# The modulation of the first norm on TensorE from row tiles of its weights, and ordinary products for the first query and key groups

## The chip, the cores and the metric

One core of a Trainium2 chip runs the whole program. The metric is device time in microseconds (us), the median of three runs. All arrays are 32-bit floats in HBM; a sequence of 512 tokens with 1024 channels goes through two transformer blocks.

## The reference, cut to what matters

Only the beginning of the first block bears on the change.

```
mod = silu(c) @ w_ada + b_ada                       # c: 1 x 1024, w_ada: 1024 x 6144
shift1, scale1, gate1, shift2, scale2, gate2 = split(mod, 6)
hmix = rmsnorm(x, g_norm1) * (1 + scale1) + shift1  # x: 512 x 1024
proj = hmix @ w_in                                  # w_in: 1024 x 11264
sb_q, sb_k, sb_v, r_q, r_k, r_v, r_g, br = split(proj, ...)   # sb_*: 1024 columns each, 16 heads of 64
```

After it come the stick-breaking attention over the 16 heads, a retention mixer, the projections, a feed-forward layer, and then the whole second block. Of `mod`, the first norm needs `shift1` and `scale1` alone: columns 0 to 2047 of `w_ada`, 8 MB.

## The kernel before, in words

Activations lie transposed: 8 tiles of 128 channels by 512 tokens. A product with a weight matrix is made in higher precision from three products (`mm3`): each operand is split into a rounded part (`hi`, made by ScalarE with a copy) and the rest (`lo`, made by a subtraction), and hi·hi, hi·lo and lo·hi are added up in PSUM. `weights` (line 167) loads 512 KB of a weight matrix (4 tiles of 128 rows, 256 columns) on SP's queue, ScalarE makes `wh` and VectorE `wl`. `gemm` (line 189) makes 256 output columns from two such loads: 2 x 8 x 3 = 48 products of 128x128 weights with 512 tokens, for the first output tile and then for the second within each load.

The beginning is written differently. It wants the first products under way while the 8 MB of `w_ada` still arrive, so it goes by channel tiles k = 0 to 7 (`arrive`, line 337). For each k it loads the 128 columns of `shift1` and the 128 of `scale1` that belong to this channel tile, all 1024 rows of them, together with the rows k of `w_in` for six output tiles: query columns 0 to 511 and key columns 0 to 255 (lines 341 and 342). `ada_part` (line 322) multiplies the 8 row tiles by `silu(c)` and adds them up on VectorE, 8 instructions of 128x256 for each k; `ada_total` (line 331) sums over the partitions with two one-column products on TensorE. A program line of TensorE with plain 32-bit operands becomes two instructions, each with its own weight load, so these are four in the trace. `modulated` (line 424) turns the sums into a factor and a shift and makes the two halves of the normed tile H[k]; for k of 2 and up GpSimd has multiplied x by the reciprocal root (`x_norm`, line 449). `w_split` (line 440) splits the rows of `w_in`: ScalarE makes the hi part, GpSimd the lo part. Then all 6 x 3 products with H[k] are issued, into six PSUM accumulators that stay open over all k (lines 467 to 469). The query tiles 0 to 3 (two groups of 256 columns) and the key tiles 0 and 1 (one group) are done when k = 7 is through.

Before that, x is loaded in four tiles of 128 tokens and turned by 32 transposes on TensorE (`x_turn`, line 350; four of the eight channel tiles before the norm's reciprocal roots are spread over the partitions, four after). The sums of squares are taken on ScalarE and VectorE, the power on GpSimd, and `spread` (line 268) makes R0 on TensorE.

After the six accumulators are emptied (`q_stack`, `k_stack`), the attention loop over the heads starts (line 617). Into it a queue of background products (`Feed`) is interleaved: the value groups, the other query and key groups and the gates. How much is put between two steps of the loop is set by hand in us (`SB_FILL`). All instructions are placed in their engines' queues when the program is built, by a scheduler that goes by the order in the program and by estimated readiness; on the chip every engine works through its own queue in that order.

Loads go through SP's queue in the order of issue. A store of x to HBM (`xspill`, 8 x 256 KB) is held until the last load of the beginning has been issued (line 474).

The steps of the prediction touch: `ada_load` (284), `ada_part` (322), `ada_total` (331), `arrive` (337), `x_turn` (350), `modulated` (424), `w_split` (440), `x_norm` (449), the loop of the first pass (459), the emptying of the accumulators (568) and the filling of the background queue (573).

Of the kernel before, what the change touches and what calls it, by code (L numbers as in the profile page):

```python
# [74 lines left out]
X_EARLY = 4  # L75
N_DIRECT = 2
# [45 lines left out]
def build(tc, A, dump=None):  # L122
    nc = tc.nc
    with ExitStack() as es:
# [64 lines left out]
        def gemm(w, kt, c0, X, evac, n0=0, k0w=0, tag="g"):  # L189

            ps = [psum(tag) for _ in range(2)]
            for b, kn in ksteps(kt, 4):
                wh, wl = weights(w, k0w + b, kn, c0, 256)
                for n, i in ((n, i) for i in range(kn) for n in range(2)) if kt == 4 else \
                        ((n, i) for n in range(2) for i in range(kn)):
                    s, k = slice(n * 128, n * 128 + 128), b + i
                    mm3(ps[n], wh[:, i, s], wl[:, i, s], X[k][0], X[k][1], b + i == 0, b + i == kt - 1)
                    if b + i == kt - 1:
                        evac(n0 + n, ps[n])
                    yield STEP  # L200
# [81 lines left out]
        w_ada4 = A["w_ada"].rearrange("(k p) (g n) -> p k g n", p=128, n=D)  # L282

        def ada_load(k, k0):

            tag = "raw" if k0 == 0 or k % 2 == 0 else "q" if k == 1 else "wl"
            n = 2 if tag == "q" else 4
            rows = []
            for j in range(k0, k0 + 4, n):
                raw = (new(tag) if n == 2 else wtile(tag, [128, 1024], F32)).rearrange("p (k n) -> p k n", n=256)  # L290
                for g in range(2):
                    nc.sync.dma_start(raw[:, :, g * 128:g * 128 + 128], w_ada4[:, j:j + n, g, k * 128:(k + 1) * 128])
                rows += [raw[:, i] for i in range(n)]
            return rows

        xr = []
        first = ada_load(0, 0)
# [39 lines left out]
        def arrive(k):  # L337

            raws = (first if k == 0 else ada_load(k, 0)) + ada_load(k, 4)
            wr = [new("q"), new("q")]  # L340
            nc.sync.dma_start(wr[0], w_in[k * 128:(k + 1) * 128, 0:512])
            last = nc.sync.dma_start(wr[1][:, 0:256], w_in[k * 128:(k + 1) * 128, 1024:1280])
            acc = new("t")[:, 0:256]
            ada_part(raws, acc)
            return acc, wr, last

        coming = [arrive(0)]
# [10 lines left out]
        for k in range(X_EARLY):  # L358
# [15 lines left out]
        for k in range(X_EARLY, KD):  # L374
            x_turn(k)
# [44 lines left out]

        H = []
        a1 = small("a1", 8)
        acc = [psum("g") for _ in range(3)] + [psum("z") for _ in range(2)] + [psum("r")]
        def modulated(k):
            ps = ada_total(coming[k][0])
            nc.vector.tensor_add(mod[:, k:k + 1], ps[:, 0:1], col("b_ada", k))
            nc.vector.scalar_tensor_tensor(out=a1[:, k:k + 1], in0=ps[:, 1:2], scalar=bsc1[:, k:k + 1],
                                           in1=col("g_norm1", k), op0=ALU.add, op1=ALU.mult)
            H.append(pair("p"))
            if k < N_DIRECT:  # L430
                norm_mod(xT[k], R0, a1[:, k:k + 1], mod[:, k:k + 1], H[k])
                return
            t = new("t")
            nc.scalar.activation(t, xn[k], AF.Identity, scale=a1[:, k:k + 1], bias=mod[:, k:k + 1])
            split(t, *H[k])

        xn = {}
        ws = {}

        def w_split(k):  # L440
            wr = coming[k][1]
            wh = wtile("wh", [128, 1024], F32R)
            wl = wtile("wl", [128, 1024], F32R)
            for r, o, n in ((wr[0], 0, 512), (wr[1], 512, 256)):
                nc.scalar.copy(wh[:, o:o + n], r[:, 0:n])
                nc.gpsimd.tensor_tensor(out=wl[:, o:o + n], in0=r[:, 0:n], in1=f(wh[:, o:o + n]), op=ALU.subtract)
            ws[k] = wh, wl

        def x_norm(k):
            if k >= N_DIRECT:  # L450
                xn[k] = new("p")
                nc.gpsimd.tensor_tensor(out=xn[k], in0=xT[k], in1=R0, op=ALU.mult)

        x_norm(0)
        w_split(0)
        modulated(0)
        x_norm(1)
        coming.append(arrive(1))
        for k in range(KD):
            if k + 2 < KD:  # L460
                coming.append(arrive(k + 2))
                x_norm(k + 2)
            if k + 1 < KD:
                w_split(k + 1)
                modulated(k + 1)
            wh, wl = ws[k]
            for n, off in enumerate((0, 128, 512, 640, 256, 384)):
                s = slice(off, off + 128)
                mm3(acc[n], wh[:, s], wl[:, s], H[k][0], H[k][1], k == 0, k == KD - 1)
        last_load = coming[-1][2]  # L470
# [97 lines left out]
        for n in (0, 1):  # L568
            ev_q(n, acc[n])
            ev_k(n, acc[2 + n])  # L570
        for n in (4, 5):
            ev_q(n, acc[n])
        for g in range(4):
            if g > 1:
                bg.add("qk%d" % g, gemm(w_in, KD, 256 * g, H, ev_q))
            if g > 0:
# [858 lines left out]
```

## Time and profile before

| | |
|---|---|
| median of 3 runs | 1952.21 us (1951.51 to 1953.27) |
| the profiled execution, its own time | 1956.69 us |
| its span (first to last instruction) | 1955.0 us |
| TensorE busy (PE) | 1879.9 us, 96% |
| weight loads (PEld, beside PE) | 1563.7 us, 80% |
| VectorE (DVE) / ScalarE (ACT) / GpSimd (POOL) | 1062.4 / 748.5 / 287.9 us |

The profile names engines PE (matrix products), PEld (weight loads of TensorE, which overlap PE), DVE, ACT, POOL and SP; a name with q is an engine's queue. A row of a timeline gives the start in us, the busy time in us, engine, line, operation, output<-inputs and, after x, how many instructions were merged. A bracket gives the idle time before it and what ended it. Ends of products are modelled and overlap, so the distance between starts is the pace, and not the duration shown. TensorE's clock has two levels, 1.2 and 2.4 GHz; PEclk is the granted share of the higher one.

### The profile page before, as it was taken

The page shows a single profiled execution, that of the slowest core. Times are in us where ns is not written, and L with a number is a line of the kernel's source. Part 1 is how long each engine was busy: PE and PEld are TensorE (multiplying, and loading weights), DVE is VectorE, ACT ScalarE, POOL GpSimd, SP SyncE. Part 2 cuts the span into 40 slices and gives each one's busy share as a digit, 9 for nine tenths or more (in the row PEclk, how much of TensorE's full clock was granted, in tenths as well). Part 3 has the DMA queues.
Part 4 walks back from the last instruction along what each step waited for, and adds up shares of the span by engine and source line. Part 5 has one row for each costly group of instructions (what it writes and reads, how often), then busy time and mean ns, then how long its engine had stood idle before and what let it go on. Part 6 is the DMA issues. An engine that isn't in the chain of part 4 may idle for free. (4 is left out here: it accounts for less than half of the span.)

```text
span 1955.0 us, 24601 instructions
## 1 busy us (share of the span) xinstructions
PE 1879.9 (96%) x9561; PEld 1563.7 (80%) x9561; DVE 1062.4 (54%) x1732; ACT 748.5 (38%) x1248; POOL 287.9 (15%) x361
## 2 busy tenths in 40 slices
PE   6889999999999999999999999979999899999998
PEld 4678887888989898888888888858888788888886
DVE  6888876645565555655334422467577554433222
ACT  3466654233332323333322222474366542223122
POOL 3232221102030302010000002122234200000000
PEclk7999999999999999999999999979999999999999
DMA  6612122533424243623333233266453123333222
GB/s 214 204 55 66 61 70 86 162 125 103 131 84 143 79 130 114 212 84 97 97 97 91 93 106 109 71 162 151 98 136 113 44 76 97 90 94 97 86 86 75
DMA packets 196400, 209.73 MB, mean 107 GB/s; under 512 B 10038, under 2 KB 179012, under 8 KB 196284
## 3 DMA queue, kind: packets, MB, share of 16 engines
q1 hardware_dynamic: 189920, 188.48, 31.6%
q0 software_dynamic: 6016, 19.57, 4.2%
q8 instruction: 75, 1.23, 0.3%
q14 instruction: 41, 0.34, 0.1%
q10 hardware_dynamic: 348, 0.13, 0.0%
HBM read 189.25 MB, written 9.99 MB: 102 GB/s over the span
## 5 line engine op out<-in xcount | busy, mean ns | idle before, releaser
L160 PE MATMUL ps_g<-p,wh 128*128 128x512 f32 (+1 forms) x1464 | 579.4, 399 | 9.3 <-DVE q L943 3.7
L161 PE MATMUL ps_g<-p,wh 128*128 128x512 f32 (+1 forms) x1464 | 576.3, 394 | 2.8 <-DVE p L415 2.8
L162 PE MATMUL ps_g<-p,wl 128*128 128x512 f32 (+1 forms) x1464 | 575.5, 394 | 0.0
L183 DVE TENSOR_TENSOR wl<-raw,wh 128x1024 fp32r<-128x1024 f32 (+1 forms) x262 | 325.9, 1244 | 447.8 <-ACT wh L182 446.6
L182 ACT CAST wh<-raw 128x1024 fp32r<-128x1024 f32 (+1 forms) x262 | 273.2, 1043 | 630.5 <-PE ps_g L161 358.3
L160 PEld LDWEIGHTS ps_g<-p,wh 128*128 128x128 f32 x1464 | 276.4, 190 | 75.1 <-issue 8.3
L162 PEld LDWEIGHTS ps_g<-p,wl 128*128 128x128 f32 x1464 | 277.2, 189 | 63.4
L161 PEld LDWEIGHTS ps_g<-p,wh 128*128 128x128 f32 x1464 | 277.4, 190 | 62.2 <-DVE p L415 3.6
L213 PE MATMUL ps_g<-wh,p 128*128 128x256 f32 x512 | 147.3, 288 | 2.0 <-ACT wh L182 1.5
L214 PE MATMUL ps_g<-wl,p 128*128 128x256 f32 x512 | 144.3, 282 | 1.2 <-DVE wl L183 1.2
L215 PE MATMUL ps_g<-wh,p 128*128 128x256 f32 x512 | 144.7, 283 | 0.0
L160 PE MATMUL ps_g<-q,wh 128*128 128x512 f32 (+1 forms) x368 | 141.7, 388 | 0.2 <-DVE p L1269 0.2
L162 PE MATMUL ps_g<-q,wl 128*128 128x512 f32 (+1 forms) x368 | 141.5, 385 | 0.0
L161 PE MATMUL ps_g<-q,wh 128*128 128x512 f32 (+1 forms) x368 | 141.5, 385 | 0.0
L213 PEld LDWEIGHTS ps_g<-wh,p 128*128 128x128 f32 x512 | 97.9, 191 | 3.3 <-ACT wh L182 1.9
L214 PEld LDWEIGHTS ps_g<-wl,p 128*128 128x128 f32 x512 | 97.9, 191 | 1.9 <-DVE wl L183 1.4
L215 PEld LDWEIGHTS ps_g<-wh,p 128*128 128x128 f32 x512 | 97.7, 191 | 0.1
L160 PEld LDWEIGHTS ps_g<-q,wh 128*128 128x128 f32 x368 | 69.1, 188 | 16.1 <-DVE p L1269 0.6
L162 PEld LDWEIGHTS ps_g<-q,wl 128*128 128x128 f32 x368 | 69.2, 188 | 15.0
L161 PEld LDWEIGHTS ps_g<-q,wh 128*128 128x128 f32 x368 | 69.2, 188 | 14.5
L150 ACT CAST q<-t 128x512 fp32r<-128x512 f32 (+1 forms) x68 | 39.1, 581 | 87.3 <-DVE t L890 48.8
L329 DVE SCALAR_TENSOR_TENSOR adaacc<-raw,cact,adaacc 128x256 f32<-128x256 f32 x112 | 53.9, 482 | 23.9 <-DMA raw<-in_w_ada 22.1
(376 smaller groups left out, 2600.7 us busy)
## 6 DMA issues: line engine op xcount, KB each, us to landing
raw<-in_w_in SPq DMA_DIRECT2D x108, 512.0 KB, 3.9
raw<-in_w_ffn_in SPq DMA_DIRECT2D x44, 512.0 KB, 3.4
raw<-in_w_ada SPq DMA_DIRECT2D x32, 512.0 KB, 3.4
raw<-in_w_ffn_gate SPq DMA_DIRECT2D x22, 512.0 KB, 3.7
raw<-in_w_ffn_up SPq DMA_DIRECT2D x22, 512.0 KB
raw<-in_w_ffn_down SPq DMA_DIRECT2D x22, 512.0 KB, 3.6
wl<-raw POOLq DMA_DIRECT2D x20, 512.0 KB, 5.6
raw<-in_w_ffn_out SPq DMA_DIRECT2D x19, 512.0 KB, 3.5
```

The costliest lines, as they stand in the source:

```text
L150: nc.scalar.copy(hi, src)
L160: nc.tensor.matmul(ps, lh, rh, start=start, stop=False)
L161: nc.tensor.matmul(ps, lh, rl, start=False, stop=False)
L162: nc.tensor.matmul(ps, ll, rh, start=False, stop=stop)
L182: nc.scalar.copy(wh, raw)
L183: low_engine["e"].tensor_tensor(out=wl, in0=raw, in1=f(wh), op=ALU.subtract)
L213: nc.tensor.matmul(o, xh[:, ts], wh[:, i], start=k == 0 and t % 2 == 0, stop=False)
L214: nc.tensor.matmul(o, xh[:, ts], wl[:, i], start=False, stop=False)
L215: nc.tensor.matmul(o, xl[:, ts], wh[:, i], start=False, stop=k == KD - 1 and t % 2 == 1)
L329: nc.vector.scalar_tensor_tensor(out=acc, in0=w, scalar=c, in1=acc, op0=ALU.mult, op1=ALU.add)
```

## The change

The first norm's modulation is summed on TensorE. For each k the kernel now loads 128 *rows* of `w_ada`, columns 0 to 2047, as four tiles of 128x512 (256 KB each, 2 KB runs). Each of the 16 blocks of 128 columns is the stationary operand of a one-column product with the k-th column of `silu(c)`; all add up in one PSUM tile of 16 columns. The sums are complete only when the last row tile is through. Then three VectorE instructions make the factors and shifts for all channels at once, and the eight tiles H[k] are made one after the other (`activation`, copy, subtraction).

The special first pass is gone: `arrive`, the VectorE sums, `modulated`, `w_split` and `x_norm`, and the six open accumulators. The first query group (256 columns) and the first key group are ordinary `gemm`s, run before the attention loop; the query group's two weight loads are issued ahead of the last two row loads of `w_ada`. The second query group goes into the background queue like the others. x is turned in one go before the roots are spread, and the eight products of x with R0 are on VectorE instead of GpSimd.

```diff
--- before.py
+++ after.py
@@ -72,8 +72,6 @@
 T_FILL = (1.8, 2.35, 0.74)
 G_FILL = 2.6
 D_FILL = (1.2, 0.87, 0.84)
-X_EARLY = 4
-N_DIRECT = 2
 
 
 class Feed:
@@ -186,11 +184,11 @@
         def ksteps(kt, step):
             return [(b, min(step, kt - b)) for b in range(0, kt, step)]
 
-        def gemm(w, kt, c0, X, evac, n0=0, k0w=0, tag="g"):
+        def gemm(w, kt, c0, X, evac, n0=0, k0w=0, tag="g", ws=None):
 
             ps = [psum(tag) for _ in range(2)]
             for b, kn in ksteps(kt, 4):
-                wh, wl = weights(w, k0w + b, kn, c0, 256)
+                wh, wl = ws[b // 4] if ws else weights(w, k0w + b, kn, c0, 256)
                 for n, i in ((n, i) for i in range(kn) for n in range(2)) if kt == 4 else \
                         ((n, i) for n in range(2) for i in range(kn)):
                     s, k = slice(n * 128, n * 128 + 128), b + i
@@ -279,22 +277,14 @@
                                      start=i == 0, stop=i == len(srcs) - 1)
 
 
-        w_ada4 = A["w_ada"].rearrange("(k p) (g n) -> p k g n", p=128, n=D)
-
-        def ada_load(k, k0):
-
-            tag = "raw" if k0 == 0 or k % 2 == 0 else "q" if k == 1 else "wl"
-            n = 2 if tag == "q" else 4
-            rows = []
-            for j in range(k0, k0 + 4, n):
-                raw = (new(tag) if n == 2 else wtile(tag, [128, 1024], F32)).rearrange("p (k n) -> p k n", n=256)
-                for g in range(2):
-                    nc.sync.dma_start(raw[:, :, g * 128:g * 128 + 128], w_ada4[:, j:j + n, g, k * 128:(k + 1) * 128])
-                rows += [raw[:, i] for i in range(n)]
-            return rows
+        def ada_load(k):
+
+            rows = [new("q") for _ in range(4)]
+            for c in range(4):
+                last = nc.sync.dma_start(rows[c], A["w_ada"][k * 128:(k + 1) * 128, c * 512:(c + 1) * 512])
+            return rows, last
 
         xr = []
-        first = ada_load(0, 0)
         for t in range(4):
             xt = wtile("wh" if t < 3 else "wl", [128, D], F32)
             nc.sync.dma_start(xt, A["x"][t * 128:(t + 1) * 128])
@@ -334,17 +324,6 @@
                 nc.tensor.matmul(ps[:, i:i + 1], acc[:, i * 128:i * 128 + 128], ones[:, 0:1], start=True, stop=True)
             return ps
 
-        def arrive(k):
-
-            raws = (first if k == 0 else ada_load(k, 0)) + ada_load(k, 4)
-            wr = [new("q"), new("q")]
-            nc.sync.dma_start(wr[0], w_in[k * 128:(k + 1) * 128, 0:512])
-            last = nc.sync.dma_start(wr[1][:, 0:256], w_in[k * 128:(k + 1) * 128, 1024:1280])
-            acc = new("t")[:, 0:256]
-            ada_part(raws, acc)
-            return acc, wr, last
-
-        coming = [arrive(0)]
         xT = []
 
         def x_turn(k):
@@ -355,7 +334,7 @@
             nc.scalar.copy(xk, ps)
             xT.append(xk)
 
-        for k in range(X_EARLY):
+        for k in range(KD):
             x_turn(k)
         ss = small("ss", 4)
         for t in range(4):
@@ -371,8 +350,29 @@
         rps = psum("r")
         spread(rps, rx)
         nc.scalar.copy(R0, rps)
-        for k in range(X_EARLY, KD):
-            x_turn(k)
+        xn = []
+        for k in range(KD):
+            xn.append(new("p"))
+            nc.vector.tensor_mul(xn[k], xT[k], R0)
+
+
+        aps = psum("o")
+        for k in range(KD):
+            if k == KD - 2:
+                w_first = [weights(w_in, b, 4, 0, 256) for b in (0, 4)]
+            rows, last_load = ada_load(k)
+            for j in range(16):
+                nc.tensor.matmul(aps[:, j:j + 1], rows[j // 4][:, (j % 4) * 128:(j % 4) * 128 + 128], cact[:, k:k + 1],
+                                 start=k == 0 and j == 0, stop=k == KD - 1 and j == 15, skip_group_check=True)
+        a1 = small("a1", 8)
+        nc.vector.tensor_add(a1, aps[:, 8:16], bsc1)
+        nc.vector.tensor_add(mod[:, 0:8], aps[:, 0:8], cols[:, VOFF["b_ada"]:VOFF["b_ada"] + 8])
+        nc.vector.tensor_mul(a1, a1, cols[:, VOFF["g_norm1"]:VOFF["g_norm1"] + 8])
+        H = []
+        for k in range(KD):
+            t = new("t")
+            nc.scalar.activation(t, xn[k], AF.Identity, scale=a1[:, k:k + 1], bias=mod[:, k:k + 1])
+            H.append(split_new(t, "p"))
 
         pending = []
 
@@ -417,57 +417,6 @@
         def pair(tag):
             return new(tag, F32R), new(tag, F32R)
 
-
-        H = []
-        a1 = small("a1", 8)
-        acc = [psum("g") for _ in range(3)] + [psum("z") for _ in range(2)] + [psum("r")]
-        def modulated(k):
-            ps = ada_total(coming[k][0])
-            nc.vector.tensor_add(mod[:, k:k + 1], ps[:, 0:1], col("b_ada", k))
-            nc.vector.scalar_tensor_tensor(out=a1[:, k:k + 1], in0=ps[:, 1:2], scalar=bsc1[:, k:k + 1],
-                                           in1=col("g_norm1", k), op0=ALU.add, op1=ALU.mult)
-            H.append(pair("p"))
-            if k < N_DIRECT:
-                norm_mod(xT[k], R0, a1[:, k:k + 1], mod[:, k:k + 1], H[k])
-                return
-            t = new("t")
-            nc.scalar.activation(t, xn[k], AF.Identity, scale=a1[:, k:k + 1], bias=mod[:, k:k + 1])
-            split(t, *H[k])
-
-        xn = {}
-        ws = {}
-
-        def w_split(k):
-            wr = coming[k][1]
-            wh = wtile("wh", [128, 1024], F32R)
-            wl = wtile("wl", [128, 1024], F32R)
-            for r, o, n in ((wr[0], 0, 512), (wr[1], 512, 256)):
-                nc.scalar.copy(wh[:, o:o + n], r[:, 0:n])
-                nc.gpsimd.tensor_tensor(out=wl[:, o:o + n], in0=r[:, 0:n], in1=f(wh[:, o:o + n]), op=ALU.subtract)
-            ws[k] = wh, wl
-
-        def x_norm(k):
-            if k >= N_DIRECT:
-                xn[k] = new("p")
-                nc.gpsimd.tensor_tensor(out=xn[k], in0=xT[k], in1=R0, op=ALU.mult)
-
-        x_norm(0)
-        w_split(0)
-        modulated(0)
-        x_norm(1)
-        coming.append(arrive(1))
-        for k in range(KD):
-            if k + 2 < KD:
-                coming.append(arrive(k + 2))
-                x_norm(k + 2)
-            if k + 1 < KD:
-                w_split(k + 1)
-                modulated(k + 1)
-            wh, wl = ws[k]
-            for n, off in enumerate((0, 128, 512, 640, 256, 384)):
-                s = slice(off, off + 128)
-                mm3(acc[n], wh[:, s], wl[:, s], H[k][0], H[k][1], k == 0, k == KD - 1)
-        last_load = coming[-1][2]
         vec_cols(1)
         show("hT", H)
         xspill = DR.tile([KD, 128, T], F32, name="xspill")
@@ -565,15 +514,11 @@
         def ev_k(n, ps):
             k_stack(ps, ks)
 
-        for n in (0, 1):
-            ev_q(n, acc[n])
-            ev_k(n, acc[2 + n])
-        for n in (4, 5):
-            ev_q(n, acc[n])
+        run(gemm(w_in, KD, 0, H, ev_q, ws=w_first))
+        run(gemm(w_in, KD, 1024, H, ev_k))
         for g in range(4):
-            if g > 1:
+            if g > 0:
                 bg.add("qk%d" % g, gemm(w_in, KD, 256 * g, H, ev_q))
-            if g > 0:
                 bg.add("qk%d" % g, gemm(w_in, KD, 1024 + 256 * g, H, ev_k))
 
             def later(g=g):
```

## Rows read from the trace of the kernel before

**Rows 1.** Windows by stage: length, busy us of each engine (instructions), clock, DMA share, GB/s.
```profile
20.00:80.00 60.00, 45.52 (x175) 32.65 (x174) 51.22 (x86) 19.18 (x35) 27.96 (x23) 0.87 0.68 214
80.00:120.00 40.00, 34.37 (x189) 28.41 (x190) 32.54 (x48) 25.13 (x52) 11.15 (x22) 0.91 0.24 72
120.00:320.00 200.00, 189.17 (x1079) 159.91 (x1079) 164.21 (x242) 121.97 (x245) 45.55 (x106) 0.99 0.21 65
```

**Rows 2.** Groups by line, 0 to 80 us: busy us, mean ns | idle before.
```profile
L329 DVE SCALAR_TENSOR_TENSOR t<-raw,cact,t 128x256 f32<-128x256 f32 x40 | 26.5, 663 | 1.0
```

**Rows 3.** Timeline, the end of the first pass and the start of the values.
```profile
79.38 0.40 PE L162 MATMUL ps_r<-p,wl 128*128 128x512 f32 x1
...
81.27 0.39 PE L213 MATMUL ps_g<-wh,p 128*128 128x256 f32 x1 [1.49 <-ACT wh L182]
...
82.87 0.39 PE L214 MATMUL ps_g<-wl,p 128*128 128x256 f32 x1 [1.21 <-DVE wl L183]
```

**Rows 4.** Timeline, four one-column products at the lower clock, and what follows them.
```profile
31.14 0.85 PE L334 MATMUL ps_o<-ones,t 128*128 128x1 f32 x4
31.78 0.31 PEld L161 LDWEIGHTS ps_z<-p,wh 128*128 128x128 f32 x1
```

**Rows 5.** Timeline, eight one-column products at the higher clock, and the next product.
```profile
440.87 0.95 PE L278 MATMUL ps_o<-ones,t 128*128 128x1 f32 x8
...
441.68 0.47 PE L160 MATMUL ps_g<-p,wh 128*128 128x512 f32 x1
```

**Rows 6.** Windows around changes of the clock, columns as in rows 1.
```profile
30.00:32.00 2.00, 2.00 (x9) 1.71 (x8) 0.48 (x1) 0.00 (x0) 0.00 (x0) 0.50 1.01 319
32.00:34.00 2.00, 1.34 (x5) 0.76 (x5) 1.94 (x6) 0.74 (x2) 0.00 (x0) 1.00 0.14 50
...
40.00:42.00 2.00, 1.05 (x6) 0.57 (x5) 1.93 (x6) 1.31 (x2) 0.00 (x0) 1.00 0.59 164
42.00:44.00 2.00, 1.82 (x4) 1.45 (x5) 1.97 (x3) 0.95 (x3) 1.22 (x1) 0.56 0.61 148
84.00:86.00 2.00, 2.00 (x12) 2.00 (x11) 1.94 (x3) 1.26 (x2) 0.00 (x0) 0.50 0.79 257
```

**Rows 7.** One line, the transposes of x: duration ns min/median/max, first and last start.
```profile
L353 PE MATMUL ps_g<-eye,wh x9: 418/418/421, 7.5 to 11.2; 128*128 128x128 f32 x9
...
L353 PE MATMUL ps_g<-eye,wl x3: 272/272/273, 13.8 to 14.1; 128*128 128x128 f32 x3
```

**Rows 8.** Windows in which the DMA engines are full, columns as in rows 1.
```profile
12.00:22.00 10.00, 4.55 (x23) 4.23 (x23) 5.24 (x12) 5.98 (x12) 2.34 (x2) 0.65 1.04 319
...
62.00:76.00 14.00, 11.81 (x51) 8.25 (x50) 10.94 (x21) 5.06 (x9) 5.12 (x5) 1.00 1.02 339
```

**Rows 9.** Timeline, from the last x tile to the spread of R0.
```profile
13.56 0.44 PE L353 MATMUL ps_r<-eye,wl 128*128 128x128 f32 x2 [1.59 <-DMA wl<-in_x]
...
16.65 0.58 PE L271 MATMUL ps_r<-eye,rx 128*128 128x128 f32 x1 [2.11 <-POOL rx L266]
```

**Rows 10.** Timeline, from the sums of k = 7 to its products.
```profile
72.77 0.60 PE L334 MATMUL ps_o<-ones,t 128*128 128x1 f32 x4 [0.99 <-DVE t L329]
...
73.24 0.48 PE L161 MATMUL ps_z<-p,wh 128*128 128x512 f32 x1
...
73.80 0.81 ACT L434 ACTIVATE t<-p,mod,a 128x512 f32<-128x512 f32 x1 [4.07 <-DVE a L427]
...
74.64 0.62 ACT L150 CAST p<-t 128x512 fp32r<-128x512 f32 x1
...
75.31 0.97 PE L160 MATMUL ps_g<-p,wh 128*128 128x512 f32 x3
...
75.47 0.68 DVE L151 TENSOR_TENSOR p<-t,p 128x512 fp32r<-128x512 f32 x1
...
76.35 0.40 PE L161 MATMUL ps_g<-p,wh 128*128 128x512 f32 x1
...
76.58 0.40 PE L162 MATMUL ps_g<-p,wl 128*128 128x512 f32 x1
```

## The prediction

> **What bounds the kernel now.** I read the windows by stage first. The kernel is a stream of products: TensorE is busy 189.2 of the 200 us from 120 us on, so a change at its beginning is worth what it moves the point from which that stream runs without gaps. The gaps are before it: in 20 to 80 us TensorE is busy 45.5 of 60 us, VectorE 51.2; in 80 to 120 us TensorE lacks 5.6 of 40 [rows 1]. Then the groups of the first 80 us: the sums of the modulation are the largest, 40 of the 56 accumulating instructions alone 26.5 us of VectorE [rows 2]. So the first pass goes at VectorE's and the loads' pace, but its 6 x 8 x 3 = 144 products lie inside that time, and they end at 79.38 + 0.40 = 79.8 us [rows 3]. That point is what I compare: everything behind it needs these 144 products in both kernels.
>
> **The parts of the change.**
>
> Loads. Both read the 8.4 MB of the modulation and 2.1 MB of x; before H[0] the new order adds only 1.05 MB of query weights. No row shows 2 KB runs of this matrix; the two stretches with full DMA engines moved 319 and 339 GB/s [rows 8]. The whole 11.5 MB take 34 to 36 us from about 2 us on, so the last row tile lands at 36 to 38 us; at the mean rate of the whole first pass, 214 GB/s [rows 1], at 56. I take 37, and it does not decide. The 32 row tiles have 32 of the 36 buffers of their kind to themselves, so no load waits for a consumer; SP's queue holds nothing that is needed earlier. The stores of x to HBM now stand behind the last row load and are over long before anyone reads them.
>
> Sums on TensorE. 8 row tiles x 16 blocks = 128 program lines, 256 weight loads with one-column products. Their pace: at the higher clock eight take 441.68 - 440.87 = 0.81 us with the next product's start, 0.10 each [rows 5], and four take 73.24 - 72.77 = 0.47, 0.12 each [rows 10]; I take 0.115. At the lower clock three loads lie between 31.14 and 31.78, 0.213 each [rows 4]. So the stream costs 256 x 0.115 = 29.4 us or 256 x 0.213 = 54.5 us. It can begin when the first row tile has landed and the queue has passed the spread of R0: the last x tile was there at 13.56 and the spread began at 16.65 [rows 9]. Half a MB of loads less ahead of x makes that some 1.6 us earlier, and the planner may put the first sums ahead of the spread; I take 14 us, with 12 and 17 as bounds. The sums wait in TensorE's queue, and what is queued behind them are all of the 144 products.
>
> The clock of this stream is the open question. What rows show: the clock came back to 1.00 at 32 us after a stretch filled with 512-column products, and fell at 42 us after 2 us with 1.05 us of work [rows 6]; the transposes of x, 128 columns each, took 418 ns until 11.2 us and 272 ns from 13.8 on [rows 7]. So a run of 128-column work was enough for the rise. No row shows a run of one-column products longer than eight; the eight are embedded in wide products and say nothing of what the clock does alone [rows 5]. Both ends are possible: 29.4 and 54.5. By columns moved, one in each 0.1 to 0.2 us, the nearest row is the window that preceded the fall, not the one that preceded the rise; by weight loads it is the transposes. I take the columns, and so the lower clock, with 2 us off because the transposes leave the clock up for the first of the sums: the sums end at T = 14 + 54.5 - 2 = 66.5 us.
>
> The Trainium skill (TensorE: Matmul & The Clock Gate, Why this matters for your kernels) speaks for the other end: keep TensorE continuously busy and the gate opens. The stream is continuously busy, so by that rule it would run at 0.115 and T would be 43.4. The same page (Part 4, PE-mode transpose) says that transposes do not count as busy in the same way; the transposes here did speed up, 418 to 272 ns [rows 7], so on that the trace disagrees.
>
> From the sums to H. Before, the sums of one k led to its first product in 75.31 - 72.77 = 2.5 us, of which 0.5 are the sums [rows 10]; so 2.0 us, three small VectorE instructions instead of two. Then ScalarE makes one tile each 75.26 - 73.80 = 1.46 us, and VectorE's half follows 0.9 us behind the copy. H[7] is whole at T + 2.0 + 7 x 1.46 + 0.9 = T + 13.1. The query group's products for its first tile run as the H tiles come, 12 products of the second tile are left behind H[7], at 0.23 each [rows 10]: T + 16.4. The key group and the second query group, 96 products, follow at 22.2 us: T + 38.6 for the same 144 products. Below it is bounded by TensorE alone, 2.0 + 144 x 0.2315 = T + 35.4; above by 1 to 2 us more if the clock is still down when H begins, which I take at 1.
>
> Removed and hidden. The 64 VectorE instructions, GpSimd's splits and its products with R0 all go; the eight products with R0 on VectorE (0.7 us each, the size of the subtraction in [rows 10]) and the two splits of the query weights lie beside the sums, which leave VectorE idle. They would cost 8 us only if the sums were through before about 25 us. More transposes before the spread cost TensorE 16 x 0.14 us, and are in the bound of 17.
>
> The start of the attention. Before, six accumulators were emptied at once and the value weights were split late: TensorE waited 1.5 and 1.2 us [rows 3] and then ran at the lower clock around 85 us [rows 6]; the mean clock of 0.91 in those 40 us [rows 1] is 3.6 us of work lost, of which I put 1.7 here. Here two groups are emptied while the next runs, so I give back 4.4 us. What is late next are VectorE's halves in the attention loop, which has 32.5 of 40 us of VectorE work already [rows 1]; so between 0 and 8.
>
> The sum: 66.5 + 38.6 + 1 - 79.8 - 4.4 = +22 us against the profiled execution's 1956.7 us (span 1955.0). The median of the runs shown is 1952.2, 4.5 below it; with the same difference I forecast 1974. Its own range: from 62 + 35.4 - 79.8 - 8 = +10 to 70 + 40.6 - 79.8 = +31, so 1962 to 1983.
>
> **The rivals.**
>
> A, the stream gets the higher clock. For it: the engine has no gap and loads weights all the time, as the transposes did [rows 7]. Against: almost no columns. T = 14 + 29.4 = 43.4, the loads are through before; 43.4 + 38.6 - 79.8 - 4.4 = -2, so 1950.
>
> B, the other side, faster. It needs the higher clock too, and then that the products are no longer paced by the H tiles: the planner fills the gaps between H tiles with products of the key group, T + 35.4, and the second query group in the background fills all 5.6 us that TensorE lacks in 80 to 120 us and wins back the lost clock there (3.6 us). 43.4 + 35.4 - 79.8 - 9 = -10: 1942. The place is TensorE's queue between 43 and 120 us; it decides only where T is below about 53, since the products need 35.4 and a gain of 9 at most stands against 79.8. Against it: the weights of the key group must be split by the ScalarE that makes the H tiles.
>
> C, the rows arrive late. At 214 GB/s [rows 1] the last of them lands at 56 us; at the higher clock T = 57 and the sum is 57 + 38.6 - 79.8 - 4.4 = +11: 1963. A stream that has the higher clock for half of its length comes out alike. For it: the loads of the first pass had that mean. Against: they waited for buffers there, and full engines moved half as much again [rows 8].
>
> **How the numbers follow.** The forecast 0.62, A 0.18, B 0.12, C 0.08. A measurement of this kernel can tell about 0.2%, 3.9 us, from no change. The forecast and C are slower by more (0.70, and I add 0.03 for A's upper end); A is mostly within (0.13) and with B makes the faster part (0.14). The range goes from 1948, which takes in over half of A, to 1984; below it lie B and the faster end of A. The likeliest case's own range is 1962 to 1983.
>
> **What would show it.** In the profile after: 256 one-column products; the distance of their starts, 0.21 us with PEclk 0.50 if I am right, 0.10 to 0.115 with 1.00 if A is. The last of them at 66 us (A: 43). The last row tile's landing at 36 to 38 us, with TensorE far behind it. From the last sum to the first product 2.0 us, then an H tile each 1.46 us. The first query and key groups through 27 us behind T. Fewer gaps in TensorE between there and the attention's steady part. The forecast is wrong if the stream's products start 0.115 us apart, or if the planner lets other products into it.

## The result, and the profile after

The kernel after takes 1971.3 us (median of 4 runs, 1967.84 to 1973.25); the kernel before, run beside it, 1952.7. The medians are 18.6 us apart; the ratio over the runs is 1.0081 [1.0064, 1.0097], which makes 15.8 us. So the kernel is slower, where +22 was forecast. The profiled execution took 1973.25 us with a span of 1971.5, against 1956.69 and 1955.0.

First the one-column products. The timeline of TensorE and its weight loads (PEld), and the line's own view, which gives durations as min/median/max, first and last start:

```profile
12.17 1.92 PE L365 MATMUL ps_o<-cact,q 128*128 128x1 f32 x16 [0.76 <-DMA q<-in_w_ada]
...
16.26 13.99 PEld L365 LDWEIGHTS ps_o<-cact,q 128*128 128x128 f32 x65
...
61.77 5.90 PE L365 MATMUL ps_o<-cact,q 128*128 128x1 f32 x27
```

```profile
L365 PE MATMUL ps_o<-cact,q x256: 212/352/352, 12.2 to 67.3; 128*128 128x1 f32 x128
```

The first 16 of the 256 come 0.12 us apart; behind the last transposes and the spread of R0 65 weight loads take 13.99 us, 0.215 each, and so it stays to the end: 16.26 + 240 x 0.214 = 67.6 us; VectorE reads the sums at 67.70. That is the price of [rows 4], not that of [rows 5]. Windows of 4 us show why (length, busy us and instructions of PE, PEld, DVE, ACT, POOL, then granted clock, DMA share, GB/s):

```profile
12.00:16.00 4.00, 3.83 (x26) 3.86 (x27) 0.00 (x0) 2.89 (x6) 0.32 (x1) 0.76 1.01 344
16.00:20.00 4.00, 4.00 (x22) 4.00 (x20) 2.67 (x5) 0.58 (x1) 0.00 (x0) 0.50 1.04 394
...
60.00:64.00 4.00, 4.00 (x20) 4.00 (x20) 0.00 (x0) 0.00 (x0) 0.00 (x0) 0.50 0.00 0
...
68.00:72.00 4.00, 2.14 (x5) 1.63 (x6) 1.76 (x5) 3.89 (x7) 0.60 (x1) 0.50 0.25 66
72.00:76.00 4.00, 4.00 (x12) 3.09 (x11) 2.15 (x4) 4.00 (x8) 0.00 (x0) 0.56 0.00 0
76.00:80.00 4.00, 4.00 (x19) 3.23 (x18) 2.92 (x4) 3.90 (x6) 0.00 (x0) 1.00 0.02 4
```

PE and PEld are busy 4.00 of 4.00 us and the clock is at 0.50, its lower level, for more than 50 us. At 60 us nothing else runs on the core: no load (the last row load was issued at 32.4 us, and they take 5.4 us to land), no other engine. Everything waits for this stream. The clock returns only at 75.5 us, behind 5 us of 512-column products.

From the sums to the attention, the timeline of all engines:

```profile
67.70 0.17 DVE L368 TENSOR_TENSOR a<-ps_o,bsc 128x8 f32<-128x8 f32 x1 [32.92 <-PE ps_o L365]
...
68.11 1.52 ACT L374 ACTIVATE t<-p,mod,a 128x512 f32<-128x512 f32 x2 [34.58 <-DVE a L370]
...
69.53 0.60 ACT L148 CAST p<-t 128x512 fp32r<-128x512 f32 x1
...
70.19 1.22 PE L158 MATMUL ps_g<-p,wh 128*128 128x512 f32 x2 [1.77 <-ACT p L148]
...
95.04 0.40 PE L160 MATMUL ps_g<-p,wl 128*128 128x512 f32 x1
95.27 0.36 PE L452 MATMUL ps_z<-q 128*128 128x128 f32 x2
```

The brackets of VectorE and ScalarE say 33 and 35 us idle until the sums. The first product comes 2.5 us after the last sum, since two activations stand ahead of the first copy. The query and key groups are through at 95.27, and the first score product (L452) follows at once. The kernel before had 14.4 us between its last product [rows 3] and its first scores:

```profile
94.14 0.41 PE L503 MATMUL ps_z<-q 128*128 128x128 f32 x2 [0.23 <-DVE q L497]
```

The windows that answer to [rows 1], of the kernel after:

```profile
20.00:80.00 60.00, 57.80 (x257) 55.53 (x258) 11.80 (x20) 13.88 (x20) 0.60 (x1) 0.54 0.48 170
80.00:120.00 40.00, 38.28 (x224) 32.79 (x223) 29.12 (x43) 21.21 (x44) 8.32 (x17) 1.00 0.31 93
120.00:320.00 200.00, 193.05 (x1100) 164.46 (x1099) 165.58 (x244) 126.44 (x251) 44.70 (x110) 0.99 0.21 67
```

In the first stage TensorE is now busy for 57.8 of 60 us, VectorE for 11.8 instead of 51.2: by busy share it looks better and is worse, because the clock is 0.54 and the work is weight loads for one column each. In the two stages behind it TensorE has fewer gaps than before (38.3 and 193.1 against 34.4 and 189.2 us).

What the two traces have in common can be compared by place (us; the branch projection is the first thing behind the attention):

| | before | after | difference |
|---|---|---|---|
| 144 products through (after: 96 at 95.3, and 48 x 0.2315) | 79.8 | 106.4 | +26.6 |
| last group of the branch projection read | 356.5 | 369.7 | +13.2 |
| squares of the final norm, the third of its eight instructions | 1878.7 | 1894.9 | +16.2 |

So the beginning cost what was forecast (66.5 + 38.6 + 1 - 79.8 = +26.3 without the give-back), and the attention gave back 13.4 us and not 4.4. Between the last two places both kernels run the same code; it took 1522.2 us before, 1525.2 after, and 1522.3 to 1525.3 in the nine other traces of this study. These 3 us belong to no step.

### The profile page after: what moved, and what is told of

Read it like the earlier page. It is cut to its first block, busy times and chain, and to the rows that moved or that the text cites. A ratio compares the mean times of both kernels' runs of the same rounds, so it can differ in the third digit from the quotient of the medians.

```text
span 1971.5 us, 24903 instructions
## 1 busy us (share of the span) xinstructions
PE 1919.9 (97%) x9785; PEld 1612.8 (82%) x9785; DVE 1026.6 (52%) x1667; ACT 748.3 (38%) x1240; POOL 257.6 (13%) x339
## 5 line engine op out<-in xcount | busy, mean ns | idle before, releaser
L158 PE MATMUL ps_g<-p,wh 128*128 128x512 f32 (+1 forms) x1488 | 590.3, 398 | 6.3 <-DVE q L888 3.7
L159 PE MATMUL ps_g<-p,wh 128*128 128x512 f32 (+1 forms) x1488 | 584.5, 393 | 0.0
L160 PE MATMUL ps_g<-p,wl 128*128 128x512 f32 (+1 forms) x1488 | 583.9, 393 | 0.0
L181 DVE TENSOR_TENSOR wl<-raw,wh 128x1024 fp32r<-128x1024 f32 (+1 forms) x268 | 333.1, 1243 | 464.3 <-ACT wh L180 463.3
L180 ACT CAST wh<-raw 128x1024 fp32r<-128x1024 f32 (+1 forms) x268 | 279.3, 1042 | 652.8 <-PE ps_g L159 376.1
L158 PEld LDWEIGHTS ps_g<-p,wh 128*128 128x128 f32 x1488 | 281.5, 190 | 71.1 <-issue 8.3
L160 PEld LDWEIGHTS ps_g<-p,wl 128*128 128x128 f32 x1488 | 281.3, 189 | 64.3
L159 PEld LDWEIGHTS ps_g<-p,wh 128*128 128x128 f32 x1488 | 281.7, 189 | 59.7 <-DVE p L149 0.7
```

The source lines that it names most:

```text
L158: nc.tensor.matmul(ps, lh, rh, start=start, stop=False)
L159: nc.tensor.matmul(ps, lh, rl, start=False, stop=False)
L160: nc.tensor.matmul(ps, ll, rh, start=False, stop=stop)
L180: nc.scalar.copy(wh, raw)
L181: low_engine["e"].tensor_tensor(out=wl, in0=raw, in1=f(wh), op=ALU.subtract)
```

## The experiments

The theory: the stream of one-column products at the lower clock sets the end, one for one, and it would have the higher clock if each weight load were followed by 128 columns instead of one. The rivals on the stream: the loads set the end anyway; or the pace is one of the weight loads, whatever the clock. On the give-back: either the second query group in the background fills gaps of the attention, or the kernel before lost time at the attention's start. Times are medians beside runs of the kernel before on the same chip, and ratios go to those.

**1. The same sums with 128 equal columns.**

```diff
-    nc.tensor.matmul(aps[:, j:j + 1], rows[j // 4][:, ...], cact[:, k:k + 1], ...)
+    nc.tensor.matmul(aps[j // 4][:, s], rows[j // 4][:, s],
+                     cact[:, k:k + 1].to_broadcast([128, 128]), ...)      # four PSUM banks
```

> The changed kernel with 128 columns in each product of the sums instead of one (the column of silu(c) repeated); same 256 weight loads, same loads from HBM; the sums lie in four PSUM banks. Theory (the products' columns decide the granted clock, and the clock sets the pace of the sums): PEclk 1.00 in the stream after its first microseconds, starts 0.115 us apart, sums complete at about 44 us instead of 67.5, first H products at the higher clock at once (2 us more): 1971 - 25 = 1946 us (1942 to 1950). Rival 1 (the weight loads of 32-bit operands pace the stream whatever is streamed behind them): starts stay 0.21 us apart, 1970 to 1975 us. Rival 2 (the row tiles' arrival sets the end of the sums): no change beyond 3 us.

Measured 1945.97 us, ratio 0.995 [0.9935, 0.9965]. TensorE computes 128 times as many columns and the kernel is 25 us faster than the kernel after, and faster than the one before. Timeline and windows of this version:

```profile
13.49 2.84 PE L366 MATMUL ps_g<-cact,q 128*128 128x128 f32 x24
...
41.19 1.05 PE L366 MATMUL ps_o<-cact,q 128*128 128x128 f32 x8
```

```profile
16.00:20.00 4.00, 4.00 (x39) 4.00 (x38) 4.00 (x7) 0.00 (x0) 0.00 (x0) 1.00 1.04 370
...
36.00:40.00 4.00, 4.00 (x38) 4.00 (x38) 0.16 (x1) 0.00 (x0) 0.00 (x0) 1.00 1.04 396
40.00:44.00 4.00, 2.51 (x22) 2.19 (x20) 1.03 (x6) 1.32 (x2) 0.60 (x1) 1.00 1.04 345
44.00:48.00 4.00, 3.24 (x10) 2.35 (x11) 2.08 (x3) 4.00 (x8) 0.00 (x0) 0.82 0.77 272
```

The windows are as full as those of the kernel after, 4.00 of 4.00; the clock is 1.00 and 38 or 39 instructions fit where there were 20 to 22. The starts are 0.112 us apart at the end (24 within 2.84 us overall), and the sums are complete at 42.2 us instead of 67.7. The weight loads are the same 256, so their pace is not fixed whatever the clock. The branch projection ends at 343.5 us, 26.2 earlier than in the kernel after, for 25.5 us less of sums. The 2 us that the expectation adds for H products at the higher clock did not come: the first of them starts at 44.76 us, and the clock falls here too (0.82 and 0.75 in the two windows from 44 to 52 us). The sums also lie in four PSUM banks instead of one; no run changes that alone.

**2. Half the sums.** The blocks that give the first shift are kept, the eight of the scale are left out and the shift's sums stand in for them.

```diff
-    for j in range(16):
+    for j in range(8):
```

> The changed kernel with 8 of the 16 blocks of each row tile in the sums; the scale's blocks are left out and the shift's sums are used for both. All loads stay. Theory (the stream lies on the path one to one, at 0.213 us for each of its instructions): 128 fewer, 27 us less, sums complete at about 41 us: 1944 us (1940 to 1949). Rival 2 (the row tiles' arrival sets the end): the last row lands at 38 us by issue time plus landing time, so also 41, told apart by when TensorE waits for rows; if they came later than that, less than 20 us gained. If the time were lost elsewhere than in the stream: less than 5 us gained.

Measured 1943.78 us, ratio 0.9936 [0.9921, 0.9951]. The stream is still at the lower clock (36 to 40 us below) and ends at 40.4 us, 27.3 earlier than in the kernel after; the time is 27.5 us less. TensorE waits for rows here, 5.6 us in all, so with half the sums the loads begin to count.

```profile
36.00:40.00 4.00, 4.00 (x20) 4.00 (x21) 0.00 (x0) 0.00 (x0) 0.00 (x0) 0.50 1.05 404
```

With the first experiment this settles the first question: the end of the sums lies on the path one for one, it is the clock that makes the stream long, and the loads, landed near 38 us, would allow an end far ahead of 67.7.

**3. The second query group ahead of the attention**, in the kernel after.

```diff
     run(gemm(w_in, KD, 1024, H, ev_k))
+    run(gemm(w_in, KD, 256, H, ev_q))
...
-    if g > 0:
+    if g > 1:
         bg.add("qk%d" % g, gemm(w_in, KD, 256 * g, H, ev_q))
+    if g > 0:
```

> The changed kernel with the second query group run ahead of the attention loop instead of in its background. Theory (most of what the change gives back in the attention, 13 us by the two traces, comes from that group filling TensorE's gaps in the loop): the gaps come back, 6 to 9 us slower, 1977 to 1980 us. Rival (what is given back is the stall at the start of the loop, six accumulators emptied at once, and the clock lost there): within 2 us of 1971.

Measured 1968.64 us, ratio 1.0062 [1.0047, 1.0077]: not slower than the kernel after, rather 3 us faster (the intervals overlap). In the traces its projection ends 6.2 us earlier, but 4.5 of them come from the stream of sums, which is the same code: here it kept the higher clock for some 5 us longer and ended at 63.2 us, in the sixth experiment at 67.6 and in the seventh at 62.8. Its last 240 products, and the window from 16 us on, which had 22 products at 0.50 in the kernel after:

```profile
15.50 47.65 PE L365 MATMUL ps_o<-cact,q 128*128 128x1 f32 x240
```

```profile
16.00:20.00 4.00, 4.00 (x36) 4.00 (x35) 3.68 (x7) 0.29 (x1) 0.00 (x0) 0.92 1.05 375
```

Whole times and places from zero carry this difference between executions; stretches behind the sums do not. So the give-back is not the second group filling gaps. With all 144 products ahead, as in the kernel before, the attention and the projection still take 15.0 us less than there. One window over that stretch each, of this version and of the kernel before:

```profile
101.80:363.50 261.70, 252.36 (x1427) 213.55 (x1426) 203.40 (x301) 148.00 (x293) 56.96 (x135) 1.00 0.25 79
```

```profile
79.80:356.50 276.70, 260.05 (x1425) 217.45 (x1426) 214.02 (x313) 155.38 (x306) 60.05 (x135) 0.98 0.24 75
```

TensorE has the same instructions (1427 and 1425 records) and is idle for 9.3 us here, 16.7 before, with 0.02 less clock on 277 us before. VectorE and ScalarE have 12 and 13 instructions more in that stretch of the kernel before, 10.6 and 7.4 us of work. Eleven of them on each engine are the emptying of its six accumulators, which lies almost wholly behind the last product there and ahead of it here.

**4. The second query group in the background**, in the kernel before.

```diff
-    for n, off in enumerate((0, 128, 512, 640, 256, 384)):
+    for n, off in enumerate((0, 128, 512, 640)):
...
-    for n in (4, 5):
-        ev_q(n, acc[n])
...
-    if g > 1:
+    if g > 0:
```

> The kernel before with the second query group's products left out of the first pass and run in the loop's background; loads and splits of the first pass stay as they are. Theory (that group fills gaps in the loop, and the first pass is paced by VectorE and the loads, so it does not get shorter): 11.1 us of products later, 9 given back: about 1955, within 4 us of 1952.7. Rival (only the stall at the start is given back, 4.4): 1959 or more.

Measured 1962.33 us, ratio 1.0033 [1.002, 1.0045]: the rival's end. Fewer products for each channel tile leave TensorE idle more often in the first pass, and its clock goes down there:

```profile
64.00:68.00 4.00, 3.19 (x8) 2.58 (x9) 3.89 (x6) 1.55 (x4) 2.35 (x2) 0.65 1.02 305
68.00:72.00 4.00, 2.40 (x11) 1.78 (x10) 3.13 (x10) 2.03 (x4) 0.00 (x0) 0.92 1.06 395
72.00:76.00 4.00, 4.00 (x14) 3.13 (x13) 3.14 (x4) 0.23 (x1) 2.35 (x2) 0.57 1.02 310
76.00:80.00 4.00, 2.67 (x10) 1.89 (x10) 1.36 (x5) 1.43 (x2) 0.61 (x1) 0.86 0.87 307
```

The pass ends at 82.7 us, 2.9 later than before with a third fewer products, and the values start at the lower clock. From there to the end of the projection it takes 282.9 us; without the 11.1 of the 48 products moved there that is 271.8, or 4.9 less than the 276.7 of the kernel before. The edit also leaves four accumulators to empty together instead of six, so it does not tell what gave these 4.9.

**5. Sharing the sums** with the idle VectorE, in the version with 128 columns: row blocks 1, 3 and 5 are scaled and added there, and their total goes through one set of products with ones.

```diff
+    if k in (1, 3, 5):
+        nc.vector.tensor_scalar(rows[c], rows[c], cact[:, k:k + 1], None, op0=ALU.mult)     # k = 1
+        nc.vector.scalar_tensor_tensor(out=aside[c], in0=rows[c], scalar=cact[:, k:k + 1],
+                                       in1=aside[c], op0=ALU.mult, op1=ALU.add)             # k = 3, 5
+        continue
```

> The version with 128 equal columns, with three of the eight row blocks (1, 3, 5) multiplied by their column of the activation and added up on VectorE, and the total put through one set of 16 products with a column of ones. That takes 2 of 8 sets of products (32 matmuls of two records, 0.224 us each: 7.2 us) off TensorE's stream, which ended at 42.2 us. Theory (the stream sets the end until the loads do): the last of the weights' rows is issued at 31.7 us and takes 5.4 to 7.1 us, so it lands at 37 to 39, and the sums end near 39; 3 us are gained, some 1943 where the version with 128 columns stands at 1946 (1941 to 1945). Rival 1, the twelve operations on VectorE (0.66 us each by the group of the first pass) come late because the norm's multiplications stand beside them: no gain, 1945 to 1948. Rival 2, TensorE pauses for rows and the clock falls to half in the stream again: slower, 1950 or more.

Measured 1946.75 us, ratio 0.9958 [0.9943, 0.9973]: no gain, by the second rival's mechanism at the first rival's price. Windows of this version:

```profile
24.00:28.00 4.00, 3.73 (x32) 3.54 (x32) 2.73 (x5) 0.00 (x0) 0.00 (x0) 1.00 1.06 373
28.00:32.00 4.00, 0.00 (x0) 0.00 (x0) 2.24 (x4) 1.21 (x2) 0.00 (x0) 0.87 1.07 369
32.00:36.00 4.00, 3.52 (x16) 3.52 (x17) 1.83 (x2) 0.89 (x1) 0.00 (x0) 0.50 1.06 392
36.00:40.00 4.00, 4.00 (x30) 4.00 (x29) 0.00 (x0) 0.00 (x0) 0.00 (x0) 0.78 1.05 404
```

With less to do TensorE waits 4.8 us for the rows of k = 6, until 32.5 us, goes on at the lower clock, and the sums end at 46.0 us: 3.8 later than with all eight row blocks on TensorE.

**6. Late emptying.** The third experiment, with the six accumulators kept until the last of the 144 products in program order.

```diff
-    run(gemm(w_in, KD, 0, H, ev_q, ws=w_first))
+    run(gemm(w_in, KD, 0, H, lambda n, ps: held.append((ev_q, n, ps)), tag="gg", ws=w_first))
...
+    for i in (0, 2, 1, 3, 4, 5):
+        held[i][0](*held[i][1:])
```

> The kernel after with the second query group's products ahead of the attention's loop (1.006 times the kernel before in the earlier run), and all six accumulators emptied only after the last product of the six, as the kernel before did. Nothing else is changed: the same products, splits and loads. Theory (the kernel before lost its time at the loop's start because its six accumulators were emptied together, 14.8 us from the last product to the first score, so that the value group's products that should fill the loop were used up before it): from the last product to the last product group of the projection 273 to 277 us as in the kernel before (276.7) where the version without the delay takes 261.7; time 1.0062 + 12/1955, about 1.012 times before, 1977 to 1983. Rival (only the two waits for the value weights' split and the lower clock behind them cost there, the 4.4 us of the prediction): 266 us, about 1.008. Rival 2 (the two traces differ by chance): no change, 1.006.

Measured 1969.85 us, ratio 1.0074 [1.0057, 1.0091], like the third. But the edit did not do what was meant: each accumulator was emptied once its own products were done, the first by VectorE at 83.28 us, 22 us ahead of the last product. The order in the program did not hold this work back. So it says nothing on the theory; it is the third experiment over again, and the stretch from the last product to the projection takes 262.2 us where that took 261.7.

**7. All six complete at once.** The same products row tile by row tile, as in the first pass of the kernel before.

```diff
+    for i in range(4):                                   # for b = 0 and 4
+        for n in range(6):
+            (wh, wl), s, k = ws[n // 2], slice(n % 2 * 128, n % 2 * 128 + 128), b + i
+            mm3(acc[n], wh[:, i, s], wl[:, i, s], H[k][0], H[k][1], k == 0, k == KD - 1)
```

> The run with the late emptying did not hold the six accumulators back: each was emptied as soon as its own products were done, the first at 83.3 us, 22 us ahead of the last product. Here the 144 products (second query group included) run row tile by row tile into six accumulators, as in the kernel before, so that all six are complete only at the last tile and are emptied together behind the last product; the modulation is that of the kernel after. Same products and evacuations; the weights come in two halves of three groups, so TensorE may pause between the halves, which is ahead of what is compared. What is compared: from the last of the 144 products to the last product group of the projection. Theory (the emptying of six accumulators at once delays the first scores and uses up the products that should fill the loop): 273 to 277 us, like the kernel before (276.7), where the run with the second group ahead took 261.7 and the one with late emptying 262.2. Rival (the kernel before lost the time otherwise: the wait for the value weights' split and the lower clock behind it): 262 to 266 us. The whole time follows from that and from the pause between the halves: 1980 to 1990 by the theory, 1970 to 1977 by the rival.

Measured 1975.29 us, ratio 1.0115 [1.0095, 1.0136], against 1.0062 [1.0047, 1.0077] for the third experiment: some 10 us, with intervals that don't meet. Timeline of TensorE, and the window over attention and projection:

```profile
101.03 0.39 PE L160 MATMUL ps_r<-p,wl 128*128 128x512 f32 x1
101.53 0.38 PE L211 MATMUL ps_g<-wh,p 128*128 128x256 f32 x1
...
113.87 0.41 PE L452 MATMUL ps_z<-q 128*128 128x128 f32 x2 [0.24 <-DVE q L446]
```

```profile
101.30:373.60 272.30, 256.81 (x1427) 214.31 (x1427) 213.05 (x314) 154.43 (x305) 59.31 (x135) 0.99 0.25 78
```

The last of the 144 products comes at the same time as in the third experiment (101.0 against 101.6 us), but the first scores wait until 113.87 for VectorE's subtractions on the key accumulators, and TensorE spends those 12.6 us on the value products that were to fill the attention's gaps. Soon they are missing: TensorE waits for ScalarE and the clock falls, as in the kernel before and not in the third experiment. First the wait and two windows of this version, then the window of the third experiment, then two of the kernel before:

```profile
128.05 0.60 PE L452 MATMUL ps_z<-q 128*128 128x256 f32 x2 [2.86 <-ACT q L559]
```

```profile
125.00:130.00 5.00, 2.14 (x8) 1.42 (x7) 4.87 (x9) 2.12 (x5) 1.21 (x3) 0.83 0.00 0
130.00:135.00 5.00, 5.00 (x23) 3.90 (x23) 2.07 (x6) 1.54 (x4) 0.00 (x0) 0.83 0.01 3
```

```profile
125.00:130.00 5.00, 5.00 (x25) 4.17 (x24) 4.50 (x7) 3.77 (x8) 2.16 (x6) 1.00 0.34 102
```

```profile
105.00:110.00 5.00, 3.46 (x17) 2.46 (x18) 4.87 (x9) 2.18 (x6) 1.89 (x5) 1.00 0.00 0
110.00:115.00 5.00, 5.00 (x19) 3.83 (x19) 2.57 (x6) 0.65 (x2) 0.00 (x0) 0.66 0.00 0
```

The stretch takes 272.3 us instead of 261.7, 15.5 us of it idle instead of 9.3, and VectorE and ScalarE have 13 and 12 instructions more in it, much as in the kernel before. The 272.3 are a little under the theory's 273 to 277 and far above the rival's 262 to 266. The whole time, though, fell into the rival's range (1970 to 1977) and 5 us under the theory's: I had allowed for a pause between the halves that did not come (38.6 us from the sums to the last product in both). The two profiled executions, whose sums end at 62.8 and 63.2 us, took 1975.16 and 1965.12, so the 10 us are in the whole time as well.

**8. Both gains together:** 128 columns and the second query group ahead of the attention.

> The version with 128 equal columns and the second query group's products ahead of the loop: both edits that gained by themselves (25 us and 2.7 us against the kernel after). Theory: they sum, 1946 - 3 = 1943 (1941 to 1946). Rival: the 2.7 us were a matter of where the slow stream left the loads (the weights were all in place by then), and with loads still arriving at 45 us the second group ahead of the loop waits: 1946 to 1950.

Measured 1943.47 us, ratio 0.9943 [0.9928, 0.9957]. It is the fastest complete version: 27 us below the kernel after and 11 below the kernel before. Against experiment 1 the intervals overlap.

**9. The same with the shared sums.**

> The version that shares the sums between VectorE and TensorE, with the second query group's products ahead of the loop. By the sum of the two expectations 1940 (1938 to 1944); by the rivals of each, no better than the version with 128 columns (1946).

Measured 1946.04 us, ratio 0.996 [0.9945, 0.9975]: no better, as experiment 5 had it.

## Why the prediction was right, point by point

- **The clock of the stream**, on which all hung. Right: 0.214 us a product where 0.213 was taken, and the end of the sums at 67.7 where 66.5 was. The stream began earlier (12.2 instead of 14), stood aside for the last transposes and the spread until 16.3, and had the higher clock only for its first 16 products. That the end came so near is partly luck: the same stream ended at 62.8 to 67.6 us in three other traces, all within the 62 to 70 of the forecast. Experiment 1 had the same loads and the same busy share with 128 columns in place of one, and the clock was 1.00 in place of 0.50. The Trainium skill (TensorE: Matmul & The Clock Gate, Why this matters for your kernels) says to keep TensorE busy without a pause to get the higher clock; here the trace disagrees for one-column products, 4.00 of 4.00 us busy at 0.50 up to 67 us.
- **The loads** were no bound, as said: issued by 32.4 us and landed near 38. They were faster than the 319 and 339 GB/s of [rows 8]: 369 to 394 from 16 to 32 us.
- **From the sums to the last of the 144 products**: T + 38.6 + 1 forecast, T + 38.7 measured, but for other reasons. The H tiles came each 1.22 us and not 1.46, since activation and copy of ScalarE overlap (0.81 + 0.60 us of records on a pace of 1.22), the first product took 2.5 us instead of 2.0, and the lower clock until 75.5 us took about 2.5 us instead of 1 (12 products in 5.3 us). From there the remaining 84 of the two groups took 19.8 us, 0.236 each, so the H tiles no longer paced them. The errors cancel.
- **The give-back at the attention's start** is the term that was mis-sized: 4.4 us with 8 as its bound, measured 13.4 by the places above. The forecast priced only the two waits of [rows 3] and the lower clock behind them. It passed over what six accumulators emptied at once do to the scores: 12 us of value products run before the scores begin and are missing later as filler. Experiments 3 and 7 give that part 10.6 us (272.3 less 261.7). The rest of the distance to the kernel before, 276.7 less 272.3, is 4.4, the size of the waits and the clock that had been counted, which the seventh experiment does not have (0.1 us between last product and values, clock 1.00). That part is a difference of traces; no run took it away alone, and the match is partly chance, since the kernel before loses clock once more farther on (0.91 from 220 to 240 us) and the seventh experiment does not. With the second group in the background the kernel after loses 1.6 of the two: 274.4 - 11.1 = 263.3 against 261.7.
- **The sum**: the forecast was +21.9. The sums ended 1.2 us later than forecast, the way from there to the last of the 144 products was 0.9 shorter and the give-back 9.0 larger, which makes the +13.2 at the projection. The 3 us by which the same code differs between executions make it +16.2 at the final norm: that these hide a third of the miss in the give-back is luck.
- **The rivals.** A and B needed the higher clock. In experiment 1 it is there, and T = 42.2 came out close to their 43.4; with the larger give-back that version is at 1946, between the 1950 and 1942 which A and B gave. C is out: the last rows landed near 38 us and not at 56.

## What to carry to other kernels

A busy TensorE is not a fast one: read the granted clock beside the busy share, and where each weight load is followed by one column, try more columns before counting on the pace; here 128 equal columns cost nothing and gave 25 us. When several accumulators become complete at the same moment, ask what waits for their emptying and what TensorE will use up meanwhile; finished one after the other, they empty beside the next one's products. And taking work off an engine whose clock depends on it can cost more than the work.

## What was not expected of the hardware

- Loads, most of them with 2 KB runs, moved 369 to 394 GB/s in the windows of 4 us from 16 to 32 us of the kernel after, against 319 and 339 in [rows 8]. The Trainium skill (DMA: Bandwidth & Descriptors, Bandwidth) has 425 GB/s for a transfer of 16 MB by one core while the other core of its pair is idle; the trace agrees so far that its windows lie below that.
- 128 columns with 32-bit operands take no longer than one, as long as each brings its own weights: 0.112 us from start to start in experiment 1 at the higher clock, against 0.10 to 0.12 for one column [rows 5, 10].
- In experiment 5 a wait of 4.8 us without a product was followed by the lower clock, although the clock had been 1.00 for 16 us before; of the same products 24 then took 5.45 us where they took 2.84.
